# A hybrid decoder layer on one core: the output projection in scaled float16 pairs that are split once, the first operands of the up projection made between its products, the down projection as one sequence of entries

## The chip, the cores and the metric

The kernel runs on one core of one Trainium2 chip, in one launch. The metric is the device time of a launch in microseconds, as the median of several runs. TensorE (PE) multiplies, VectorE (DVE) and ScalarE (ACT) work element by element, GpSimd (POOL) does some elementwise work and issues some transfers, SyncE (SP) issues most DMA transfers. Each engine works through its own list of instructions in order.

## What is computed

One layer on 2048 tokens of width 1024, in float32. The reference, cut to what matters here:

```python
h = rmsnorm(x, norm1_g) * (1 + sc1) + sh1
proj = h @ w_in
q, k, v, fg, xin, bg, cg = jnp.split(proj, IN_SPLITS, axis=-1)
...
attn = forgetting_attention(q, k, v, logf).reshape(b, s, ATTN_WIDTH)
conv = bg * causal_dwconv(cg * xin, conv_mix_w)
mixed = jnp.concatenate([attn, conv], axis=-1)
x = x + g1 * (mixed @ w_out)

h2 = rmsnorm(x, norm2_g) * (1 + sc2) + sh2
u = causal_dwconv(h2 @ w_up, ffn_conv_w)
u_gate, u_val = jnp.split(u, 2, axis=-1)
y = (jax.nn.silu(u_gate) * u_val) @ w_down
return x + g2 * y
```

Attention has 8 heads of 64 over a width of 512, the convolution the other 512 channels; w_out is 1024 x 1024, w_up 1024 x 5632, w_down 2816 x 1024.

## The kernel before, in words

A float32 product is made as three products of halves: each operand is split into a high part (ACT, a copy to the narrower type) and a low part (DVE, the operand less the high part), and `mm3` (L141) issues high x high, high x low and low x high. In the projections and in the output and down projections the halves are of type fp32r, in the up projection float16. A matmul has a stationary tile of 128 x 128 and streams 512 columns.

The program runs through these stages: the norm of x, the input projection (`project`, first K, then Q, then the convolution's channels), attention in 64 steps of two query blocks, the output projection, norm 2, and then twice (hv = 0, 1, half of the rows each) the up projection with the gated convolution, and the down projection.

**The output projection** (`mixed`) has 64 entries: four groups Q of 512 rows, two halves hf of the columns, eight slices k of the depth. For each entry `split` (ACT L720, DVE L721) splits the gated slice of w_out and the slice of the mixed rows anew, 128 splits of 128x512 in all, and four row tiles t take one `mm3` each: 768 matmuls. The first eight entries run under the last steps of attention. At the end of a half the sum is added to x on DVE (L792) and POOL stores the rows (L794, L796) to `x1_sc` in DRAM.

**Norm 2** (`norm2`) makes the up projection's operands. `columns` transposes four 128x128 blocks on PE into PSUM (L1047), ACT applies scale and shift (L1049), `operand` splits into float16 halves (L1037, L1038). Rows of groups 0 and 1 are normalised on POOL (L1075), those of 2 and 3 on DVE (L1077). Its generator is advanced at chosen entries of `mixed`: 18 steps in the output projection. Four more steps, `norm2_rest`, which transposes four column sets a second time, are advanced inside the first iteration of `up(0)`.

**The up projection** (`up`) takes 22 iterations per half, one for each pair of column blocks, and makes the 2048-row product by a scheme with seven products instead of eight: `product` (L1167) issues 12 matmuls each. The weights of iteration i + 1 are loaded (SP, L1126) and made during iteration i: scaled on ACT (L1132), added and subtracted on DVE (L1107, L1108), split by ACT (L1111) and DVE (L1114). Those of iteration 0 are made at the head of `up`. ACT copies the first product's sum (p1, L1216) before the next product goes on accumulating in the same place; DVE adds (L1107); the convolution's taps are on ACT (L1175) and DVE (L1180); `finish` of iteration i runs in iteration i + 1, that of the last one behind the loop.

**The down projection** (`down`) is called four times for each half, 22 entries each; an entry loads a slice of y and of w_down (SP, L1262, L1263), splits both (L720, L721) and feeds four row tiles. At the end each row tile is multiplied by the gate and added to the rows, which are loaded from `x1_sc` at that point (L1026, L1028, L1029). In the first half norm2(2) and norm2(3) follow the first two calls.

**The order of the work.** K(...) pins an instruction: pinned instructions of one engine keep the order of the program text. All others are placed by a scheduler that looks at priorities and at when operands are ready. In `before` the splits of `mixed` and `down`, their additions and most of norm 2 are not pinned. Loads and splits are written right ahead of the products that use them. `magnitudes` loads a tile of w_up and adds up its magnitudes on ACT (L590) for the up projection's scale; 88 of these are spread through the input projection.

## Time and profile before

| | us |
|---|---|
| three runs | 2500.55, 2510.44, 2511.32 |
| their median | 2510.44 |
| the profiled execution, its own time | 2507.0 |
| span of its instructions | 2505.3 |
| PE busy | 2388.9 (95%) |
| DVE busy | 1814.0 (72%) |
| ACT busy | 1292.5 (52%) |
| POOL busy | 375.4 (15%) |

The span runs from the first to the last instruction of the trace; the profiled execution is 1.7 us longer. The median of the runs lies 3.4 us above the profiled execution. Busy shares are means over all stages. The attention steps lie before 962 us, the output projection from there to 1169 us, `up(0)` from 1169 to 1577 us, `down(0)` to 1849 us, `up(1)` to 2241 us, `down(1)` to the end.

### The profile page before, as it was taken

The page shows a single profiled execution, that of the slowest core. Times are in us where ns is not written, and L with a number is a line of the kernel's source. Part 1 is how long each engine was busy: PE and PEld are TensorE (multiplying, and loading weights), DVE is VectorE, ACT ScalarE, POOL GpSimd, SP SyncE. Part 2 cuts the span into 40 slices and gives each one's busy share as a digit, 9 for nine tenths or more (in the row PEclk, how much of TensorE's full clock was granted, in tenths as well). Part 3 has the DMA queues.
Part 4 walks back from the last instruction along what each step waited for, and adds up shares of the span by engine and source line. Part 5 has one row for each costly group of instructions (what it writes and reads, how often), then busy time and mean ns, then how long its engine had stood idle before and what let it go on. Part 6 is the DMA issues. An engine that isn't in the chain of part 4 may idle for free. (4 is left out here: it accounts for less than half of the span.)

```text
span 2505.3 us, 38577 instructions
## 1 busy us (share of the span) xinstructions
PE 2388.9 (95%) x14432; PEld 1655.5 (66%) x14432; DVE 1814.0 (72%) x3377; ACT 1292.5 (52%) x2068; POOL 375.4 (15%) x314
## 2 busy tenths in 40 slices
PE   4999999999899889998999999999999999999999
PEld 4988778888677667776444444678764444447887
DVE  7567784342899887676888988667859888885554
ACT  3533443210788776554656566355545555553333
POOL 4210001011577873110000000000000000000000
PEclk9999999999999999999999999999999999999999
DMA  8444786433789997143222222567742222235775
GB/s 237 148 123 127 196 238 182 147 112 89 149 173 184 189 183 196 72 140 123 67 85 85 92 85 93 191 214 235 219 142 92 84 93 84 85 122 168 230 228 186
DMA packets 429348, 368.71 MB, mean 147 GB/s; under 512 B 184336, under 2 KB 328040, under 8 KB 428136
## 3 DMA queue, kind: packets, MB, share of 16 engines
q1 hardware_dynamic: 421976, 349.40, 50.0%
q10 hardware_dynamic: 4752, 8.46, 0.9%
q0 software_dynamic: 2432, 8.39, 0.9%
q8 instruction: 113, 1.85, 0.3%
q14 instruction: 75, 0.61, 0.1%
HBM read 267.54 MB, written 65.08 MB: 133 GB/s over the span
## 5 line engine op out<-in xcount | busy, mean ns | idle before, releaser
L1167 PEld LDWEIGHTS <-pair 128*128 128x128 f16 x3696 | 364.5, 99 | 470.2 <-issue 36.4
L1167 PE MATMUL acc<-t,pair 128*128 128x512 f16 x2112 | 482.5, 382 | 6.5 <-DVE t L1107 6.5
L1167 PE MATMUL acc<-b,pair 128*128 128x512 f16 x1584 | 372.5, 386 | 17.2 <-DVE pair L1114 6.6
L141 PE MATMUL acc<-hi 128*128 128x512 f32 x960 | 378.5, 395 | 7.9 <-ACT hi L720 5.7
L141 PE MATMUL acc<-hi,lo 128*128 128x512 f32 x960 | 375.8, 391 | 0.2 <-DVE lo L721 0.2
L141 PE MATMUL acc<-lo,hi 128*128 128x512 f32 x960 | 375.1, 391 | 0.0
L721 DVE TENSOR_TENSOR lo<-raw,hi 128x1024 fp32r<-128x1024 f32 (+1 forms) x208 | 236.3, 1142 | 178.8 <-ACT hi L720 178.6
L720 ACT ACTIVATE hi<-raw 128x1024 fp32r<-128x1024 f32 (+1 forms) x208 | 204.9, 991 | 240.4 <-PE acc L141 207.7
L1180 DVE SCALAR_TENSOR_TENSOR w<-w,fcw,w 128x1024 f32<-128x1024 f32 x176 | 226.1, 1285 | 39.9 <-ACT w L1175 30.8
L141 PEld LDWEIGHTS acc<-hi 128*128 128x128 f32 x960 | 180.7, 188 | 48.2 <-ACT hi L720 6.8
L141 PEld LDWEIGHTS acc<-hi,lo 128*128 128x128 f32 x960 | 180.6, 188 | 39.7 <-DVE lo L721 1.5
L141 PEld LDWEIGHTS acc<-lo,hi 128*128 128x128 f32 x960 | 180.6, 188 | 37.0 <-DVE lo L721 0.8
L1111 ACT ACTIVATE pair<-raw 128x1024 f16<-128x1024 f32 x132 | 138.2, 1049 | 70.9 <-DVE raw L1108 70.9
L1175 ACT ACTIVATE w<-w,fcw 128x1024 f32<-128x1024 f32 x88 | 100.7, 1144 | 131.9 <-DVE w L1107 131.9
L879 ACT ACTIVATE s_t<-s_t,nb,cst 128x2048 f32<-128x2048 f32 (+15 forms) x128 | 164.7, 1288 | 5.7
L1114 DVE TENSOR_TENSOR pair<-raw,pair 128x1024 f16<-128x1024 f32 x132 | 160.7, 1219 | 3.9 <-ACT pair L1111 3.9
L590 ACT ACTIVATE wx<-wx 128x512 f32<-128x512 f32 x88 | 55.6, 632 | 202.1 <-DMA wx<-in_w_up_dram 192.5
L141 PE MATMUL pr<-hh,wh 128*128 128x512 f32 x384 | 153.9, 401 | 0.0
L141 PE MATMUL pr<-hh,wl 128*128 128x512 f32 x384 | 151.5, 394 | 2.1 <-DVE wl L178 2.1
L141 PE MATMUL pr<-hl,wh 128*128 128x512 f32 x384 | 151.6, 395 | 0.0
L891 POOL TENSOR_TENSOR wide<-s_t,wide 128x1024 f16<-128x1024 f32 x64 | 136.8, 2138 | 5.3
L862 DVE CUSTOM_DVE_ANT_0 s_t<-ps,nf,mx 128x512 f32<-128x512 f32 (+1 forms) x192 | 119.2, 643 | 16.3 <-PE ps L841 8.0
(278 smaller groups left out, 4568.6 us busy)
## 6 DMA issues: line engine op xcount, KB each, us to landing
raw<-in_w_up_dram SPq DMA_DIRECT2D x88, 512.0 KB, 3.7
raw<-y_sc SPq DMA_DIRECT2D x176, 256.0 KB, 4.3
raw<-in_w_down_dram SPq DMA_DIRECT2D x176, 256.0 KB, 4.3
wx<-in_w_up_dram SPq DMA_DIRECT2D x88, 256.0 KB, 2.8
y_sc<-w SPq DMA_DIRECT2D x44, 512.0 KB, 2.6
wm<-in_w_ada_dram SPq DMA_DIRECT2D x128, 128.0 KB, 2.9
wr<-in_w_in_dram SPq DMA_DIRECT2D x40, 256.0 KB, 4.2
x_t<-in_x_dram SPq DMA_DIRECT2D x16, 512.0 KB, 5.3
```

What stands on the lines that cost most here:

```text
L141: ins = T.matmul(acc, lhsT=a, rhs=b, start=st, stop=sp)
L590: K(A.activation(t, t, AF.Abs, accum_out=l1[:, n : n + 1]))
L720: A.activation(hi, raw, AF.Copy, scale=HS)
L721: V.tensor_tensor(lo, raw, hi.bitcast(F32), op=ALU.subtract)
L862: K(V.tensor_tensor_reduce(out=s_t[:, o0 + c0 : o0 + c0 + cw], in0=ps[:, 0:cw], in1=nf[:, c0 : c0 + cw], scale=1.0, scalar=-3.0e38 if g == ...
L879: K(A.activation(cols, cols, AF.Exp, bias=nb[:, p : p + 1], scale=qk[:, 4:5], accum_out=un["l"][:, p : p + 1]))
L891: K(G.tensor_tensor(wide[:, 1, :], s_t[:, WB * P : WU], wide[:, 0, :], op=ALU.subtract))
L1111: K(A.activation(hi, raw, AF.Copy))
L1114: K(V.tensor_tensor(lo, raw, hi, op=ALU.subtract))
L1167: K(T.matmul(acc, lhsT=a, rhs=b, start=st, stop=sp, skip_group_check=True))
L1175: K(A.activation(y, u[:, 0:1024], AF.Copy, scale=fcw[:, ct : ct + 1]))
L1180: K(V.scalar_tensor_tensor(y, u[:, m : m + 1024], fcw[:, m * 44 + ct : m * 44 + ct + 1], y, op0=ALU.mult, op1=ALU.add))
```

## The change

**Scaled float16 pairs.** `scaled_pair` splits a 128x512 slice into float16 halves after a multiplication by a power of two (ACT L771, DVE L772). The gated w_out is split once (16 slices), the mixed rows once for each group (32 slices): 48 splits instead of 128. `prepare` runs three entries ahead of the products. The addition to x takes the inverse scale in the same DVE instruction (L812); x is loaded for every group as whole rows (L801), and POOL stores 16 whole row tiles of 512 KB (L814).

**The scales.** w_out is loaded and gated four attention steps earlier (steps 28 to 59), and ACT adds up its magnitudes there, one slice in every second step (L736, 16 instructions). DVE takes the largest magnitude of each block of the convolution's result (16 reductions). `out_scales` works out the scales in attention's steps 61 to 63.

**The input projection.** `magnitudes` is left out in three of K's row tiles and three of Q's, and two more are called in the convolution's blocks.

**Norm 2** is pinned throughout, cut into 36 steps, normalises on DVE alone (L1100), and makes `b22` and `t4` with the others; the second transposition goes away. One step is taken per entry of the output projection from entry 17 on; the five steps of the first weights (`first_weights`) follow in the same chain.

**Up and down.** The first weights have a tile of their own; the last iteration of `up` loads and splits the first three pairs of `down`. `down` is one sequence of 88 entries for each half, pinned, with loads six and splits three entries ahead; the rows of the last addition are loaded three entries before the end of a group. The finish of the last `up` iteration, norm2(2), norm2(3) and the next first weights are steps between its entries.

```diff
-                    if k == 3:
+                    if k == 3 and lull[0] <= i < lull[1]:
                         magnitudes()
...
+        last_k = project(AW, gq[:, 1:2], k_hi, k_lo, {0: largest_gains, 1: gain_scales, 3: running_sum, 5: running_offset, 7: largest_value, 9: value_scale}, (0, 13))
+        last_q = project(0, gq[:, 0:1], q_hi, q_lo, {0: last_k, 1: last_k, 3: piece, 6: piece, 9: piece, 12: piece, 15: piece}, (2, 15))
...
+                V.tensor_reduce(vmax[:, 4 * j + ch : 4 * j + ch + 1], y, axis=AX.X, op=ALU.max, apply_absolute_value=True)
...
+        return (
+            lambda: K(G.tensor_tensor(t, t, gates[:, n0 : n0 + 512], op=ALU.mult)),
+            lambda: K(A.activation(wo["junk"][:, 0:512], t, AF.Abs, accum_out=sums[:, n : n + 1])),
...
+    def scaled_pair(tile, raw, scale):
+
+        hi, lo = tile[:, 0:512], tile[:, 512:1024]
+        K(A.activation(hi, raw, AF.Copy, scale=scale))
+        K(V.scalar_tensor_tensor(lo, raw, scale, hi, op0=ALU.mult, op1=ALU.subtract))
+        return hi, lo
+
+    def prepare(Q, hf, i):
+
+        k = order[i]
         if Q == 0:
+            if i % 2 == 0:
+                wp["two"] = fq.tile([P, 2048], F16, tag=("hi", "lo")[hf], name="wp", bufs=4)
+            n0 = i % 2 * 1024
+            wp[k, hf] = scaled_pair(wp["two"][:, n0 : n0 + 1024], wo[k, hf], osc[:, 1:2])
+        if hf == 0:
+            mp[Q, k] = scaled_pair(fb.tile([P, 1024], F16, tag=f"wo{k}{Q % 2}", name="mp"), src[Q, k], osc[:, 0:1])
+            if Q < 3:
+                load_mixed(Q + 1, i)
+
+    def mixed():
+
+        todo = [(Q, hf, i) for Q in range(4) for hf in range(2) for i in range(8)]
+        ready = 0
+        for n, (Q, hf, i) in enumerate(todo):
...
+            while ready < min(n + 3, 64):
+                prepare(*todo[ready])
+                ready += 1
+            if hf == 0 and i == 2:
+                kept[Q] = [wide_temp()[:, 0:D] if Q == 1 else raw_tile() for _ in range(4)]
+                for xp, r in zip(kept[Q], rows):
+                    K(nc.sync.dma_start(xp, x[r, :]))
+            if i == 0:
+                acc = [ps_d.tile([P, 512], F32, tag="d", name="acc") for _ in range(4)]
+            if i != 6:
+                for t in range(4):
+                    for e in (i,) if i < 7 else (6, 7):
+                        a, b = [m[:, t * P : (t + 1) * P] for m in mp[Q, order[e]]]
+                        mm3(acc[t], a, b, *wp[order[e], hf], e == 0, e == 7)
+            if i == 7:
+                for t in range(4):
+                    xp = kept[Q][t][:, n0 : n0 + 512]
+                    K(V.scalar_tensor_tensor(xp, acc[t], oinv, xp, op0=ALU.mult, op1=ALU.add))
+                    if hf:
+                        G.dma_start(x1_sc[Q * 4 + t], kept[Q][t])
+            yield
...
-            if s >= (H - 4) * nu and s % 2 == 0 and s < H * nu:
-                gated = load_out((s - (H - 4) * nu) // 2)
+            if s % 2 == 0 and 28 <= s < 60:
+                gated.append(load_out((s - 28) // 2))
...
+            if s == 61:
+                slow.append(out_scales(ps_x))
...
+            if 28 <= s < 60 and s % 2:
+                gated[-1][0]()
+            if 30 <= s <= 60 and s % 2 == 0:
+                gated[(s - 30) // 2][1]()
...
+            K(A.activation(hi, raw, AF.Copy))
+            K(V.tensor_tensor(lo, raw, hi, op=ALU.subtract))
...
+                for t in range(4):
+                    K(nc.sync.dma_start(xn[Q][t], x1_sc[Q * 4 + t]))
+                yield
...
+                if t % 2:
+                    yield
...
-                    V.tensor_scalar(xn[Q][t], xn[Q][t], ss[:, t : t + 1], None, op0=ALU.mult)
-            yield
+                K(V.tensor_scalar(xn[Q][t], xn[Q][t], ss[:, t : t + 1], None, op0=ALU.mult))
+                if t % 2:
+                    yield
...
+                yield
+                yield
...
-                if Q == 3:
-                    last_operands(Q, k)
-                yield
-
-        def norm2_rest(Q):
-            for k in range(4):
-                operand("b22", k, columns(Q, 4 + k))
+                yield
                 last_operands(Q, k)
...
-            raws = raw_tile(), raw_tile()
+            raws = [raw_tile() if i else fp.tile([P, 1024], F32, tag="first", name="raw", bufs=2) for _ in range(2)]
...
+        def first_weights():
...
+            wts = up_weights(0)
+            ready["ops"] = next(wts)
+            ready["wts"] = wts
+            for _ in range(5):
+                next(wts)
+                yield
...
+        def load_pair(n, i):
...
+        def first_pairs(hv):
+
+            for i in range(3):
+                raws[4 * hv, i] = load_pair(4 * hv, i)
+            yield
+            for i in range(3):
+                pairs[4 * hv, i] = split_pair(raws.pop((4 * hv, i)))
+                yield
+            while True:
+                yield
...
-            wts = up_weights(0)
-            ops = next(wts)
-            for _ in range(5):
-                next(wts)
+            wts, ops = ready.pop("wts"), ready.pop("ops")
...
-                    (ps_d.tile([P, 512], F32, tag="d", name="acc") if i % 2 else ps_u.tile([P, 512], F32, tag="u", name="acc"))
+                    (ps_u.tile([P, 512], F32, tag="u", name="acc") if i % 2 else ps_d.tile([P, 512], F32, tag="d", name="acc"))
...
-                wts = up_weights(i + 1) if i + 1 < NPAIR else iter([None] * 9)
+                wts = up_weights(i + 1) if i + 1 < NPAIR else first_pairs(hv)
...
-            for _ in last:
+            return last
...
+        def down(hv, side):
...
+            todo = [(n, i) for n in range(4 * hv, 4 * hv + 4) for i in range(NPAIR)]
+            loaded = split = 3
+            for e, (n, i) in enumerate(todo):
...
+                while split < min(e + 3, len(todo)):
+                    if loaded == split:
+                        raws[todo[loaded]] = load_pair(*todo[loaded])
+                        loaded += 1
+                    pairs[todo[split]] = split_pair(raws.pop(todo[split]))
+                    split += 1
+                while loaded < min(e + 6, len(todo)):
+                    raws[todo[loaded]] = load_pair(*todo[loaded])
+                    loaded += 1
+                if i == 0:
+                    acc = [ps_d.tile([P, 512], F32, tag="d", name="acc") for _ in range(4)]
+                if i == NPAIR - 3:
+                    xs = [fb.tile([P, 512], F32, tag=f"src{n % 2 * 4 + t}", name="xs") for t in range(4)]
+                    for xp, r in zip(xs, rows):
+                        K(nc.sync.dma_start(xp, x1_sc[r.start // P][:, n0 : n0 + 512]))
...
+                if e < 3 or e % 2 == 0:
+                    next(side, None)
+                if i == NPAIR - 1:
+                    for t in range(4):
+                        add_gated(acc[t], gates[:, D + n0 : D + n0 + 512], xs[t], out[rows[t], n0 : n0 + 512])
+            for _ in side:
                 pass
...
+        steps = {Q: norm2(Q) for Q in range(4)}
+        weights = first_weights()
+        early = chain(steps[0], (None for _ in range(4)), steps[1], weights)
+        for n, _ in enumerate(mix, 8):
+            if n >= 17:
+                next(early, None)
+        for _ in early:
-            up(hv, iter(()) if hv else norm2_rest(1))
+            last = up(hv)
+            down(hv, last if hv else chain(last, steps[2], steps[3], first_weights()))
```

The order of instructions, at three places. ACT at the start of `up(0)`, before (L1132 scales a weight tile of iteration 1, L1216 copies p1, L1049 and L1037 make operands of `norm2_rest`, L1111 splits weights):

```order
L1111 ACTIVATE pair<-raw 128x1024 x2
L1049 ACTIVATE t_15027<-pt,sh_137,a_136 128x512
L1037 ACTIVATE b_15029<-t_15027 128x512
L1037 ACTIVATE t_15036<-t_15032 128x512
L1132 ACTIVATE raw<-raw,cst 128x1024 x2
L1216 ACTIVATE t_15054<-acc 128x512
L1221 ACTIVATE w_15056<-halo 128x2
L1049 ACTIVATE t_15077<-pt,sh_137,a_136 128x512
L1037 ACTIVATE b_15079<-t_15077 128x512
```

and in the change (L1152 scales, L1271 is p1, L1130 splits weights):

```order
L1058 ACTIVATE t_14710<-t_14706 128x512
L1152 ACTIVATE raw<-raw,cst 128x1024 x2
L1130 ACTIVATE pair<-raw 128x1024
L1130 ACTIVATE pair<-t_14739 128x512
L1130 ACTIVATE pair<-raw 128x1024 x2
L1152 ACTIVATE raw<-raw,cst 128x1024 x2
L1271 ACTIVATE t_14862<-acc 128x512
L1276 ACTIVATE w_14864<-halo 128x2
L1276 ACTIVATE w_14865<-halo 128x2
L1284 ACTIVATE w_14864<-acc 128x512
```

The operands of norm 2 are gone from between the copies; the two scale operations of iteration 1 still stand ahead of p1.

SP at the same place, in the change, with what each row waits for (DMASW are transfers that POOL issued, here the stores of `x1_sc`; L801 loads x of group 3, L1146 loads w_up, the third and fourth L1146 row those of iteration 1):

```order
L801 DMA raw<-in_x_dram 128x1024 [waits DMAHW5_49,DMASW3_49,DVE_49]
L1146 DMA raw<-in_w_up_dram 128x8x128 [waits DVE_49]
L1146 DMA raw<-in_w_up_dram 128x8x128 [waits DMAHW1_49,DMAHW6_49,DMASW4_49,DVE_49]
L1146 DMA raw<-in_w_up_dram 128x8x128 [waits DMAHW2_49,DMAHW7_49,DMASW5_49,DVE_49]
L1146 DMA raw<-in_w_up_dram 128x8x128 [waits DMAHW0_49,DVE_49]
```

and before:

```order
L1126 DMA raw<-in_w_up_dram 128x8x128 [waits DMAHW2_49,DVE_49]
L1126 DMA raw<-in_w_up_dram 128x8x128 [waits DMAHW4_49,DVE_49]
L1126 DMA raw<-in_w_up_dram 128x8x128 [waits DMAHW5_49,DVE_49]
```

The loads of iteration 1 now go to tiles that hold rows of group 3, so they wait for the stores of its first two row tiles.

DVE in the last iteration of `up(0)`, before (L721 splits pairs of `down`, L1107 and L1108 are additions and subtractions of `up`):

```order
L721 TENSOR_TENSOR lo<-raw,hi 128x1024
L1108 TENSOR_TENSOR raw<-t_17956,raw 128x512
L721 TENSOR_TENSOR lo<-raw,hi 128x1024
L1108 TENSOR_TENSOR raw<-raw 128x512
L1114 TENSOR_TENSOR pair<-t_17956,pair 128x512
L1107 TENSOR_TENSOR t_18032<-t_17957,acc 128x512
L1107 TENSOR_TENSOR w_17966<-t_18032,t_18018 128x512
```

and in the change (L1198 splits, L1126 adds, L1239 taps, L1251 the product of the two halves of u):

```order
L1126 TENSOR_TENSOR t_17875<-t_17851,acc 128x512
L1198 TENSOR_TENSOR lo<-raw,hi 128x1024
L1251 TENSOR_TENSOR w_17853<-w_17806,w_17853 128x1024
L1198 TENSOR_TENSOR lo<-raw,hi 128x1024 x2
L1126 TENSOR_TENSOR t_17930<-t_17851,acc 128x512
L1126 TENSOR_TENSOR w_17860<-t_17930,t_17916 128x512
```

Three splits remain ahead of the additions, at written places; the weights of the next `up` no longer stand among them.

## Rows read from the trace of the kernel before

**Rows 1.** The page, busy time of the engines over the span.

```profile
PE 2388.9 (95%) x14432; PEld 1655.5 (66%) x14432; DVE 1814.0 (72%) x3377; ACT 1292.5 (52%) x2068; POOL 375.4 (15%) x314
```

**Rows 2.** Chain of waits, a piece of down(1): start us, us, what.

```profile
2382.65 114.09 PE acc L141 x501
```

**Rows 3.** Timeline of PE, mid up(0): start us, us, operation, [idle before <-releaser].

```profile
1385.55 2.75 PE L1167 MATMUL acc<-b,pair 128*128 128x512 f16 x12
1388.14 2.75 PE L1167 MATMUL acc<-t,pair 128*128 128x512 f16 x12
```

**Rows 4.** Windows, output projection: stretch, us, PE PEld DVE ACT POOL, PEclk, DMA, GB/s.

```profile
991.00:1169.27 178.27, 169.41 (x759) 136.99 (x757) 119.16 (x204) 96.73 (x166) 23.50 (x31) 0.99 0.37 128
```

**Rows 5.** Timeline of PE, an idle stretch of the output projection.

```profile
1085.75 0.50 PE L141 MATMUL acc<-hi 128*128 128x512 f32 x1 [1.99 <-ACT hi L720]
```

**Rows 6.** Windows: the first 60 us of up(0), and 60 us in its middle.

```profile
1169.27:1229.27 60.00, 46.41 (x193) 20.50 (x193) 46.59 (x60) 32.16 (x47) 0.91 (x2) 0.86 0.18 58
1380.00:1440.00 60.00, 60.00 (x280) 27.20 (x279) 53.91 (x62) 35.45 (x53) 0.00 (x0) 1.00 0.27 88
```

**Rows 7.** Timeline of PE: end of up(0), start and end of up(1).

```profile
1572.79 4.42 PE L1167 MATMUL acc<-t,pair 128*128 128x512 f16 x10 [3.18 <-DVE t L1107]
...
1852.74 4.45 PE L1167 MATMUL acc<-b,pair 128*128 128x512 f16 x10 [3.58 <-DVE pair L1114]
...
2236.83 4.44 PE L1167 MATMUL acc<-t,pair 128*128 128x512 f16 x12 [3.35 <-DVE t L1107]
```

**Rows 8.** Windows around these three places.

```profile
1560.00:1580.00 20.00, 16.82 (x66) 6.86 (x65) 19.21 (x21) 9.79 (x14) 0.00 (x0) 0.83 0.56 177
1849.16:1889.16 40.00, 36.42 (x156) 15.99 (x157) 30.56 (x38) 19.75 (x27) 0.00 (x0) 0.91 0.26 81
2200.00:2240.00 40.00, 36.65 (x165) 16.25 (x163) 36.48 (x41) 24.94 (x33) 0.00 (x0) 0.97 0.42 132
```

**Rows 9.** Windows: K to Q projection, the convolution's blocks, attention.

```profile
240.00:260.00 20.00, 15.98 (x72) 11.97 (x70) 14.74 (x56) 10.50 (x24) 1.88 (x3) 1.00 0.58 157
260.00:280.00 20.00, 19.87 (x84) 15.82 (x85) 13.27 (x46) 8.90 (x19) 1.85 (x3) 0.91 0.71 191
...
380.00:420.00 40.00, 40.00 (x179) 32.70 (x178) 15.73 (x32) 10.48 (x28) 3.63 (x5) 1.00 0.54 163
...
680.00:700.00 20.00, 18.71 (x291) 14.43 (x289) 18.99 (x62) 17.10 (x34) 12.92 (x8) 1.00 0.94 154
```

**Rows 10.** Timeline of PE, idle stretches at the start of up(0).

```profile
1172.85 3.82 PE L1167 MATMUL acc<-b,pair 128*128 128x512 f16 x10 [2.97 <-DVE pair L1114]
1184.63 5.17 PE L1167 MATMUL acc<-b,pair 128*128 128x512 f16 x12 [4.50 <-ACT t L1216]
1201.97 5.03 PE L1167 MATMUL acc<-b,pair 128*128 128x512 f16 x12 [6.12 <-ACT t L1237]
```

**Rows 11.** Timeline of ACT at the start of up(0), scale operations and p1.

```profile
1181.93 2.17 ACT L1132 ACTIVATE raw<-raw,cst 128x1024 f32<-128x1024 f32 x2
1184.01 0.57 ACT L1216 ACTIVATE t<-acc 128x512 f32<-128x512 f32 x1
```

**Rows 12.** DMA issues: out<-in, engine, count, KB each, median us to landing.

```profile
raw<-in_w_up_dram SPq DMA_DIRECT2D x88, 512.0 KB, 3.7
...
x_sc<-raw POOLq DMA_DIRECT2D x4, 512.0 KB, 3.4
...
x_sc<-w POOLq DMA_DIRECT2D x4, 512.0 KB, 5.9
```

**Rows 13.** Timeline of PE, idle stretches in down, first and last of five.

```profile
1669.34 0.30 PE L1047 MATMUL pt<-ident,w 128*128 128x128 f32 x1 [1.13 <-DVE w L1077]
...
2382.65 0.50 PE L141 MATMUL acc<-hi 128*128 128x512 f32 x1 [0.50 <-DVE t L1028]
```

**Rows 14.** Lines by shape, L590 on ACT: count, ns min/median/max, first and last start.

```profile
L590 ACT ACTIVATE wx<-wx x88: 627/632/636, 162.6 to 506.6; 128x512 f32<-128x512 f32 x88
L590 ACT ACTIVATION_READ_ACCUMULATOR wx<-wx x88: 183/187/195, 163.2 to 507.2; 128x1 f32 x88
```

213 lines of the change are left out of this document (78 added, 135 removed).

## The prediction

> **What bounds the kernel now.** The page's busy times come first: PE is busy 95% of the span, DVE 72%, ACT 52% [rows 1]. So time can only be won in two ways: the matmuls themselves get faster, or PE's gaps close. The chain of waits and the timeline give the pace of an undisturbed stream. For fp32r halves it is 114.09 us for 501 matmuls, 227.7 ns each [rows 2]; for float16 halves twelve matmuls start 2.59 us after the twelve before, 215.8 ns each [rows 3]. The gaps are read from the timeline, each with the instruction that ended it, and from windows, where the number of matmuls against an undisturbed stretch also shows what a lowered clock cost. A single number for idle time would miss that: after a long gap the granted clock stands below 1 for a while.
>
> The places with gaps are the output projection (8.9 us of 178.3 without PE, granted clock 0.99 [rows 4]), where PE waits for ACT's splits [rows 5]; the first 60 us of up(0), clock 0.86 [rows 6]; the ends of both ups and the start of up(1) [rows 7, 8]; and the passage from K's projection to Q's [rows 9]. In mid up PE never stops: 280 matmuls in 60 us [rows 6].
>
> **The change part by part.**
>
> *Float16 in the output projection.* 768 matmuls go from 227.7 to 215.8 ns [rows 2, 3]: 768 x 11.9 ns = **9.1 us** won. This is on the path, as PE is the bound there. The stream of [rows 3] alternates weight loads and matmuls of 512 columns, as the new output projection will. The Trainium skill, "TensorE: Matmul & The Clock Gate", section "Back-to-back issue gap", gives about 131 ns for each matmul of just such a sustained stream, by which this term would be 768 x (227.7 - 131) = 74 us, 65 more. The trace does not agree with it, so the measured pace stays in the sum.
>
> *Splits once and three entries ahead.* The gaps and the clock of this stage cost 8.86 us idle and (1 - 0.99) x 178 = 1.8 us, some 10.6 [rows 4]. 48 splits take the place of 128, and an entry's operands are asked for about 3 x 2.6 us before its products. I take **10 us** won. The stage may keep half of it, if the pinned steps of norm 2 hold up a split: the bounds are 5 and 10.6. The first entries carry extra: three pairs must be made, and the scales known, before the first product. This is work of a few hundred ns each beside attention's last steps; I charge 1 us, between 0 and 4.
>
> *Start of up(0).* 193 matmuls run in its first 60 us, of which 16 are the transpositions of four column sets; 177 products against 280 [rows 6] are 103 x 214 ns = 22.1 us lost. Three gaps account for 2.97 + 4.50 + 6.12 = 13.6 of that [rows 10], the rest is the lower clock and the transpositions. The first gap ends on the first weights, the others on ACT copies that stand in ACT's order behind operands of norm 2. With the operands and first weights made earlier, these three causes go. A new one comes: the two scale operations of iteration 1 still stand ahead of p1 (2.17 and 0.57 us [rows 11]), and their loads now wait for stores of x1. The chain behind the second row tile's addition is a store of 3.4 to 5.9 us, a load of 3.7 us [rows 12], the two scale operations and p1: 9.8 to 12.3 us. It begins some 2 us before the projection's last product, since the last twelve products (2.6 us) belong to the tiles behind it. PE has two products of 12, 5.2 us, until it needs p1's copy. So p1 is 2.7 to 5.2 us late; I take the middle, 4.0, and a third of the clock's loss that came with three gaps, (22.1 - 13.6 - 1.7) / 3 = 2.3, where 1.7 is 16 transpositions at about half a matmul. That leaves 6.3, and **15.8 us** won. Bounds: no gap (22.1 won), and a second gap like the third of [rows 10] with its clock loss on top (6.1 + 2.3 = 8.4 less).
>
> *Ends of up and start of up(1).* At the end of up(0) PE idles 3.18 us [rows 7], and 66 matmuls in 20 us against 93.3 [rows 6, 8] are 5.9 us. At up(1)'s start 156 against 186.7 in 40 us are 6.6; at its end 165 against 186.7 are 4.6 [rows 8]. All three end on DVE operations [rows 7], and DVE's order there has splits of the down projection, or weights, ahead of the additions that PE waits for. The new order makes the first weights during down(0), and the first pairs at written places. I take **6 + 6 + 4.6 = 16.6 us**; what could stay is half of the two ends, 5.
>
> *Down.* Five gaps of PE at the passages between its calls are 1.13 + 0.40 + 1.02 + 0.41 + 0.50 ([rows 13], the first and the last of the five), 3.5 us in all. **3.5 us** are won. They end on DVE: the normalised rows, and the gating at the end of a group, which waits for rows loaded only then. Both are asked for earlier now. What was unpinned is pinned, so side steps can delay a split, but splits run three entries, 8 us, ahead.
>
> *Input projection.* Between K and Q PE idles 4.0 of 20 us and the clock stands at 0.91 in the next 20 [rows 9]: 4.0 + 1.8 = 5.8. The change takes `magnitudes` out of this passage; I take **5 us**, between 0 and 5.8. The two put in their place lie in the convolution's blocks, where PE has no gap (40.00 of 40) and ACT is busy 10.5 of 40 us [rows 9]. The same row hides the 16 new reductions on DVE, 15.7 of 40 busy there.
>
> *Sums of w_out's magnitudes.* 16 operations on ACT in attention, 632 + 187 ns by the nearest row [rows 14], 13.1 us in all. Attention has DVE busy 19.0, PE 18.7 and ACT 17.1 of 20 us [rows 9]: ACT has slack but not at every moment. A fifth to a quarter shows: 3 us lost, between 0 and 13.1. The loads and gating of w_out only move four steps, on SP and POOL.
>
> **The sum**: 9.1 + 10 - 1 + 15.8 + 16.6 + 3.5 + 5 - 3 = 56.0. The profiled execution took 2507.0, so it becomes 2451.0; that execution lies 3.4 below the median of the runs.
>
> **The rivals.**
>
> 1. *Up(0) starts as late as before*: the three gaps come back with other names (scale operations behind x1's stores, p1 behind them). For it: the waits in SP's order. Against it: two of the three gaps had norm 2's operands for cause, and these are gone. Then only the transpositions' 1.7 us are won there: 2451 + 14.1 = 2465.
>
> 2. *ACT becomes the bound in attention*: all 16 sums show, 10.1 more: 2461. For it: 17.1 of 20 us. Against it: DVE is fuller.
>
> 3. *The change does not do what it says*: float16 streams no faster in this stage than fp32r, since its tiles and places in memory differ from those of up. 2451 + 9.1 = 2460. Against it: the stream of [rows 3] has the same shape.
>
> 4. *Slower.* The pinned steps of norm 2 stall PE, as the four in up(0) did. There they came with 22.1 - 1.7 = 20.4 us, 5.1 each [rows 6]. Now 36 stand pinned between the entries of the output projection, and every one puts several DVE and ACT operations ahead of the splits. At that price the gain of 56 is gone from the 11th stalled step on; all 36 would give 2451 + 184 = 2635. Against it: 18 such steps in the same stage before came with no more than the 10.6 us of that whole stage [rows 4], 0.6 each, and DVE is busy 119 of 178 there, ACT 97.
>
> 5. *The stream is paced by its weight loads alone*: they take 27.20 us for 279, 97.5 ns each [rows 6]. If the matmuls of the output projection overlapped so far, 768 x (215.8 - 97.5) = 91 us more would be won: 2360. Against it: PE has nothing else to wait for in [rows 3] and keeps 215.8. The page named above points this way, with 131 ns and so 2386.
>
> **How the numbers follow.** The forecast of 2451 has 0.69, rival 1 0.13, rival 2 0.08, rival 3 0.04, rival 4 0.05, rival 5 0.01. A measurement of this kernel tells about 0.5%, 12.6 us, from no change, so faster means below 2498. All cases but rival 4 lie there: faster 0.95. Rival 4 with 9 to 13 stalled steps is no change, 0.02, with more slower, 0.03.
>
> The range's lower end takes the forecast with no gap at up(0) (-6.3), free sums (-3) and start (-1), the last of the output projection's and the K to Q passage's gaps (-0.6 and -0.8) and the spread of the runs below the profiled execution (2507.0 - 2500.6 = 6.4): 2507.0 less 56.0, 6.3, 3, 1, 1.4 and 6.4 is 2433, and 2430 with a little for idle time in other stages. The upper end takes rival 1 (+14.1), half of the output projection's gaps (+5), half of the ups' ends (+5) and the spread above (2511.3 - 2507.0 = 4.3), or rival 2 with two of these: 2478. Outside lie rivals 4 and 5, 0.06, and about 0.1 of the tails.
>
> **What would show it.** Right: the output projection with some 216 ns per matmul and hardly a gap; up(0) beginning with one gap before the second product with b21, ended by ACT's p1, of 3 to 5 us; no gap of over 1 us at the ends of up; some 25 matmuls more than the 72 + 84 of the 40 us between K and Q; attention longer by 0 to 5 us. Wrong: gaps in the output projection that end on a split with norm 2's operations ahead of it on the same engine; two or more gaps at up(0); attention's steps longer wherever a sum of magnitudes stands; gaps in down ended by a split.

## The result and the profile after

The changed kernel takes 2469.53 us (median of 4 runs, 2467.69 to 2473.61) against 2508.31 (4 runs, 2500.55 to 2511.32): ratio 0.9852, 95% interval 0.9826 to 0.9879, some 39 us or 1.5% less. The forecast of 2451 had 56 us. The time lies in the range, the way is right, and a third of the expected gain did not come.

The profiled execution of the change has a span of 2467.1 us against 2505.3. The place of each stage's first matmul in the timelines says where the 38.2 us lie. (The stage boundaries named ahead of the prediction, 1577 and 2241 us, are the last gaps inside up; by the timeline up(0) ends at 1596.2 and up(1) at 2259.1, and that is used here.)

| stage | before | after | won | forecast |
|---|---|---|---|---|
| up to the first score of attention | 634.4 | 633.2 | 1.2 | 5 |
| attention and output projection | 534.9 | 531.0 | 3.9 | 15.1 |
| up(0) | 426.9 | 406.2 | 20.7 | 21.8 |
| down(0) | 252.3 | 253.9 | -1.6 | 3.5 with down(1) |
| up(1) | 410.5 | 398.7 | 11.8 | 10.6 |
| down(1) | 246.2 | 244.2 | 2.0 | see down(0) |

Both ups came as forecast. Of the missing part 15 us lie ahead of them and 3.1 in the two downs. The page's busy times, which answer to [rows 1]:

```profile
PE 2364.3 (96%) x14419; PEld 1585.8 (64%) x14419; DVE 1790.0 (73%) x3333; ACT 1256.6 (51%) x2016; POOL 358.6 (15%) x298
```

PE's timeline, the pace of the output projection and all its gaps of over 1 us from the end of attention to up(0) (start us, us, operation, idle before and what ended it):

```profile
966.11 0.21 PE L954 MATMUL po<-v,near 128*128 128x64 f16 x1 [4.37 <-DVE at L962]
973.88 2.74 PE L142 MATMUL acc<-wp,mp 128*128 128x512 f16 x6 [2.69 <-ACT mp L771]
...
1103.88 10.52 PE L142 MATMUL acc<-wp,mp 128*128 128x512 f16 x48
1114.24 0.60 PE L1068 MATMUL pt<-ident,w 128*128 128x128 f32 x4
1117.78 4.03 PE L142 MATMUL acc<-wp,mp 128*128 128x512 f16 x12 [2.94 <-DVE raw L812]
...
1143.43 16.81 PE L142 MATMUL acc<-wp,mp 128*128 128x512 f16 x77 [1.18 <-DVE raw L812]
...
1175.41 4.22 PE L1226 MATMUL acc<-b,pair 128*128 128x512 f16 x12 [5.89 <-ACT t L1271]
```

Forty-eight matmuls take 1114.24 - 1103.88 = 10.36 us, 215.8 ns each: the pace of [rows 3] to the digit. So the float16 term is there, and the loss stands in the brackets. None of these five waits ends on a split of a pair that was asked for too late, except the second, at the very start. Windows of the same places as [rows 6, 8, 9] (stretch, us, PE, PEld, DVE, ACT, POOL, clock, DMA share, GB/s):

```profile
240.00:260.00 20.00, 17.26 (x75) 13.63 (x74) 14.70 (x53) 9.02 (x20) 2.60 (x4) 0.92 0.52 132
260.00:280.00 20.00, 18.98 (x87) 14.97 (x86) 16.84 (x60) 8.31 (x15) 1.85 (x3) 0.99 0.62 171
...
1164.90:1224.90 60.00, 54.11 (x245) 24.17 (x244) 41.40 (x49) 30.05 (x44) 0.53 (x1) 0.94 0.38 117
1560.00:1580.00 20.00, 20.00 (x92) 12.67 (x91) 16.40 (x17) 10.35 (x13) 0.00 (x0) 1.00 0.50 158
1824.40:1864.40 40.00, 40.00 (x187) 18.13 (x185) 32.49 (x38) 20.37 (x28) 0.00 (x0) 1.00 0.21 70
2200.00:2240.00 40.00, 40.00 (x184) 24.47 (x182) 30.05 (x30) 18.11 (x22) 0.00 (x0) 1.00 0.53 164
```

The last three are gapless, at full clock. Up(0)'s first 60 us have 245 matmuls against 280: 35 x 214 ns = 7.5 us lost, where 22.1 were. Between K and Q 75 + 87 = 162 matmuls run against 72 + 84 = 156 [rows 9]: hardly any of the 5 us came.

### The profile page after: what moved, and what is told of

Read it like the earlier page. It is cut to its first block, busy times and chain, and to the rows that moved or that the text cites. A ratio compares the mean times of both kernels' runs of the same rounds, so it can differ in the third digit from the quotient of the medians.

```text
span 2467.1 us, 38327 instructions
## 1 busy us (share of the span) xinstructions
PE 2364.3 (96%) x14419; PEld 1585.8 (64%) x14419; DVE 1790.0 (73%) x3333; ACT 1256.6 (51%) x2016; POOL 358.6 (15%) x298
## 4 chain that ended last, share of the span: by engine, by line
PE 77%; DVE 7%; DMA 6%; issue 5%; ACT 3%; POOL 1%; SPq 1%; ACTq 0%; DVEq 0%; POOLq 0%
PE acc L1226 32%; PE acc L142 24%; PE pr L142 10%; PE pv L142 3%; DMA far<-wide 3%; PE pt L918 1%; PE ps L857 1%; PE ps L858 1%; DVE near L925 1%; PE po L954 1%; DVE s_t L881 1%; DMA wx<-in_w_up_dram 1%; PE po L956 1%; PE po L955 1%; ACT s_t L898 1%
## 5 line engine op out<-in xcount | busy, mean ns | idle before, releaser
L1226 PE MATMUL acc<-b,pair 128*128 128x512 f16 x1584 | 364.9, 380 | 5.9 <-ACT t L1271 5.9
L1198 DVE TENSOR_TENSOR lo<-raw,hi 128x1024 fp32r<-128x1024 f32 x176 | 211.7, 1223 | 141.9 <-ACT hi L1197 141.1
L142 PE MATMUL acc<-hi 128*128 128x512 f32 x704 | 276.9, 393 | 3.4 <-DVE t L1049 3.4
L142 PE MATMUL acc<-lo,hi 128*128 128x512 f32 x704 | 274.3, 390 | 0.3 <-DVE lo L1198 0.3
L142 PE MATMUL acc<-hi,lo 128*128 128x512 f32 x704 | 274.2, 389 | 0.0
L1197 ACT ACTIVATE hi<-raw 128x1024 fp32r<-128x1024 f32 x176 | 181.8, 1054 | 163.8 <-PE acc L142 131.1
L1239 DVE SCALAR_TENSOR_TENSOR w<-w,fcw,w 128x1024 f32<-128x1024 f32 x176 | 226.1, 1285 | 34.6 <-ACT w L1234 25.3
L142 PE MATMUL acc<-wp,mp 128*128 128x512 f16 x768 | 172.2, 383 | 6.9 <-DVE raw L812 4.1
L1130 ACT ACTIVATE pair<-raw 128x1024 f16<-128x1024 f32 x132 | 138.2, 1049 | 69.1 <-DVE raw L1127 69.1
L1133 DVE TENSOR_TENSOR pair<-raw,pair 128x1024 f16<-128x1024 f32 x132 | 160.8, 1219 | 6.8 <-ACT pair L1130 6.8
L142 PEld LDWEIGHTS acc<-hi 128*128 128x128 f32 x704 | 132.1, 188 | 34.1 <-DVE t L1049 5.5
L142 PEld LDWEIGHTS acc<-hi,lo 128*128 128x128 f32 x704 | 132.2, 188 | 27.7
L142 PEld LDWEIGHTS acc<-lo,hi 128*128 128x128 f32 x704 | 132.2, 188 | 27.4 <-DVE lo L1198 0.7
```

What stands on the lines that cost most here:

```text
L142: ins = T.matmul(acc, lhsT=a, rhs=b, start=st, stop=sp)
L1130: K(A.activation(hi, raw, AF.Copy))
L1133: K(V.tensor_tensor(lo, raw, hi, op=ALU.subtract))
L1197: K(A.activation(hi, raw, AF.Copy))
L1198: K(V.tensor_tensor(lo, raw, hi.bitcast(F32), op=ALU.subtract))
L1226: K(T.matmul(acc, lhsT=a, rhs=b, start=st, stop=sp, skip_group_check=True))
```

## The experiments

Stage lengths below are from the first matmul of a stage to that of the next, in each kernel's own timeline. One caution holds for all: stages ahead of the output projection vary between executions with the same code. Attention's 64 normalisations (the DVE line that writes `at`, one for each step) run from 656.1 to 981.7 us in the trace of before and from 654.5 to 985.1 in that of the first experiment below, which has the same attention: 325.6 against 330.6. In the traces that have the change's attention they take 333.8 (the change itself) to 342.8 us, and the first score comes at 628.4 to 637.1 us where the code up to it is the change's. So a verdict on a part rests on its own stage, not on the total alone.

Where attention varies can be read from the same line, and its end does not:

| from normalisation to normalisation, us | before | float16 alone | change | no scales | two orders | four orders |
|---|---|---|---|---|---|---|
| 1st to 49th | 251.4 | 257.1 | 250.8 | 255.5 | 255.8 | 252.9 |
| 49th to 57th | 39.8 | 39.8 | 40.4 | 40.4 | 40.4 | 46.0 |
| 57th to 64th | 34.4 | 33.7 | 42.6 | 37.7 | 42.7 | 37.8 |

The 57th and the 64th, in the kernel before and in the change:

```profile
947.29 0.29 DVE L943 TENSOR_TENSOR at<-po,l 128x128 f32<-128x128 f32 x1
981.68 0.28 DVE L943 TENSOR_TENSOR at<-po,l 128x128 f32<-128x128 f32 x1
```

```profile
946.80 0.29 DVE L962 TENSOR_TENSOR at<-po,l 128x128 f32<-128x128 f32 x1
989.38 0.29 DVE L962 TENSOR_TENSOR at<-po,l 128x128 f32<-128x128 f32 x1 [1.58 <-PE po L956]
```

In the eight traces with the scales at steps 61 to 63 the last row is 42.4 to 43.6. So the end of attention became some 8 us longer by the change, and of these the scales make up some 5: without them it takes 37.7. The other 3 were not tried apart; the first pairs are made there.

**Float16 alone, in the kernel before.**

```diff
-                (mh, ml), (wh, wl) = halves(pair_tiles())
-                split(wo[k, hf], wh, wl)
-                split(src[Q, k], mh, ml)
+                (mh, ml), (wh, wl) = halves([fq.tile([P, 2048], F16, tag=n, name=n, bufs=4) for n in ("hi", "lo")])
+                for raw, hi, lo in ((wo[k, hf], wh, wl), (src[Q, k], mh, ml)):
+                    A.activation(hi, raw, AF.Copy)
+                    V.tensor_tensor(lo, raw, hi, op=ALU.subtract)
```

> The kernel before with one part of the change alone: the pairs of the output projection are float16 (unscaled), still split 128 times at the old places. Theory 'the pace is the float16 gain': 768 matmuls at 216 instead of 227 ns, 8 to 9 us less than before (2508.3 to about 2500), and the stalls of the output projection that end on splits stay (8 to 10 us). Rival 'the splits bound this stage': PE waits longer for the same splits, and less than 3 us is won.

Measured: 2499.96 against 2510.64 in the same session, ratio 0.9963 (0.9948 to 0.9978), 5.5 to 13 us. The largest wait on a split is still there, as in [rows 5]:

```profile
996.15 0.39 PE L141 MATMUL acc<-hi 128*128 128x512 f16 x1 [2.13 <-ACT hi L769]
```

The ratio comes to 9.3 us, so the float16 term of 9.1 us is confirmed apart from all else in the change. In its own stage, from the first product to up(0), it is 196.4 us instead of 203.0, 6.6 less, since PE's waits there grew from 9.0 to 10.8 us.

**No scales to work out.** The constant 1 takes the place of `out_scales`.

```diff
-            if s == 61:
-                slow.append(out_scales(ps_x))
+            if s == 30:
+                G.memset(osc, 1.0)
+                G.memset(oinv, 1.0)
```

> The changed kernel without working out the scales of the output projection: they are the constant 1, and the twelve DVE and two PE operations of attention's last steps are left out; the sums of w_out's magnitudes on ACT and the reductions of the convolution's blocks stay. Theory 'the scales stand in DVE's order ahead of the last scores': PE's idle 4.4 us at the end of attention shrinks to below 2, the wait of 2.7 us for the first pairs stays, and the time falls by 3 to 4 us from the 2469.5 of the change. Rival 'the first pairs are late whatever the scales': the idle time moves to the first product, which then waits 5 us or more, and the time stays within 1 us.

Measured: 2467.27 (2465.68 to 2469.27), ratio to before 0.9833 (0.9813 to 0.9853); span 2463.9, 3.2 less. PE's timeline at the end of attention:

```profile
962.65 0.19 PE L954 MATMUL po<-v,near 128*128 128x64 f16 x1 [1.54 <-DVE at L962]
...
969.39 0.61 PE L142 MATMUL acc<-wp,mp 128*128 128x512 f16 x2 [3.20 <-ACT mp L771]
```

In the kernel before, the first of these waits was

```profile
962.06 0.19 PE L935 MATMUL po<-v,near 128*128 128x64 f16 x1 [1.68 <-DVE at L943]
```

The first wait falls from 4.37 to 1.54, what before had there; the second stays, a little longer. The first theory holds for both waits; the median is 2.3 us lower where it had 3 to 4. What it leaves is a start that waits 3.2 us for pairs in any case. Where the 4.9 us at the end of attention (42.6 to 37.7) come from is in the trace of the change: the twelve small DVE operations take 4.6 us in all, 1.97 of them in one. DVE and POOL at that place:

```profile
960.68 0.26 DVE L755 TENSOR_SCALAR rim<-rim 128x2 int32<-128x2 int32 x1
960.97 0.17 DVE L756 RECIPROCAL rim<-rim 128x2 f32<-128x2 f32 x1
961.17 1.97 DVE L757 TENSOR_SCALAR rim<-rim 128x2 int32<-128x2 int32 x1
...
963.65 0.73 DVE L881 CUSTOM_DVE_ANT_0 s_t<-ps,nf,mx 128x512 f32<-128x512 f32 x1
```

```profile
960.99 2.12 POOL L910 TENSOR_TENSOR wide<-s_t,wide 128x1024 f16<-128x1024 f32 x1
```

The same masking of 256 numbers takes 0.26 us at 960.68 and 1.97 at 961.17, and the second ends at 963.14, with POOL's operation (963.11). The scores (L881) stand behind it. This is taken up again in the last experiment.

**p1 ahead of the weights' scale operations.**

```diff
-                wts = up_weights(i + 1) if i + 1 < NPAIR else first_pairs(hv)
-                ops = next(wts)
                 p1 = temp()
                 K(A.activation(p1, X, AF.Copy))
+                wts = up_weights(i + 1) if i + 1 < NPAIR else first_pairs(hv)
+                ops = next(wts)
```

> The changed kernel with two statements of the up projection in the other order: the copy p1 is issued before the next iteration's weights are begun, so that it stands ahead of their two scale operations on ACT. Theory 'p1 is late because it stands behind the scale operations, which wait for w_up, which waits for stores of x1': the 5.9 us of idle and the slow clock behind it at the start of up(0) go, 7 us less (2469.5 to about 2462.5). Rival 'the weights of iteration 1 are late anyway': PE waits at a later product of iteration 0 or 1 for a weight pair or an addition, 4 to 6 us, and no more than 3 us are won.

Measured: 2484.30 (2482.68 to 2486.70), 15 us slower than the change. The gap at up(0)'s start is gone as expected, but neither theory had what came instead. PE waits in 41 of the 44 iterations, on the addition of p1 and Y:

```profile
1258.33 2.75 PE L1226 MATMUL acc<-t,pair 128*128 128x512 f16 x12 [0.33 <-DVE t L1126]
1276.95 2.75 PE L1226 MATMUL acc<-t,pair 128*128 128x512 f16 x12 [0.33 <-DVE t L1126]
```

An iteration takes 1276.95 - 1258.33 = 18.62 us. In the change p1 comes every 18.13 us, by ACT's timeline:

```profile
1265.14 0.60 ACT L1271 ACTIVATE t<-acc 128x512 f32<-128x512 f32 x1
1283.27 0.60 ACT L1271 ACTIVATE t<-acc 128x512 f32<-128x512 f32 x1
```

44 x 0.49 = 21.6 us lost, 7 won: 14.6. By the stages up(0) takes 3.1 and up(1) 9.8 us longer, 12.9; the rest of the 15 lies ahead of the ups, in what varies between executions. The scale operations head the weights' chain (ACT scales, DVE adds and subtracts, ACT and DVE split), and DVE's later additions for PE stand behind that chain in its order. An order that costs once at the start pays 44 times in the loop.

**Additions freed from norm 2's steps.**

```diff
-        early = chain(steps[0], (None for _ in range(4)), steps[1], weights)
+        early = chain(steps[0], steps[1], weights)
         for n, _ in enumerate(mix, 8):
-            if n >= 17:
+            if n >= 17 and n % 8 != 6 and not 30 <= n < 31:
```

> The changed kernel with norm 2's steps kept away from the last entry of each half in the output projection (no step after the seventh of eight entries; the four empty steps between the two groups are used up instead). Theory 'the additions at the end of a half stand behind norm 2's pinned operands on DVE, whose ACT halves come late': the waits of 2.9 and 1.2 us that end on these additions go, with the slow clock behind them 4 to 6 us less than 2469.5. Rival 'the additions wait for the accumulators themselves, since only four exist': the waits stay, within 1 us.

Measured: 2461.84 (2457.23 to 2465.61), ratio to before 0.9805 (0.9778 to 0.9833), 7.7 less than the change. Windows, the change first, then this kernel:

```profile
1080.00:1160.00 80.00, 74.23 (x352) 35.02 (x350) 50.84 (x75) 28.60 (x42) 2.12 (x4) 0.98 0.21 79
```

```profile
1080.00:1160.00 80.00, 78.56 (x378) 37.22 (x377) 56.78 (x86) 29.93 (x44) 3.11 (x6) 1.00 0.27 100
```

PE's idle time in these 80 us falls from 5.8 to 1.4 us. From the output projection's first product to up(0) it is 183.6 us instead of 190.3. The first theory holds. In the change DVE's timeline shows the place: the pinned split of a norm 2 operand waits for its ACT half, and the four additions that free the accumulators follow it all at once.

```profile
1115.70 0.69 DVE L1059 TENSOR_TENSOR t<-t,t 128x512 f16<-128x512 f32 x1 [0.69 <-ACT t L1058]
1116.31 0.75 DVE L772 SCALAR_TENSOR_TENSOR mp<-src,rim,mp 128x512 f16<-128x512 f32 x1
1116.98 2.72 DVE L812 SCALAR_TENSOR_TENSOR raw<-acc,rim,raw 128x512 f32<-128x512 f32 x4
```

**No sums of w_out's magnitudes.**

```diff
-            if 30 <= s <= 60 and s % 2 == 0:
-                gated[(s - 30) // 2][1]()
+            if s == 30:
+                G.memset(sums, 16.0)
```

> The changed kernel without the sixteen sums of w_out's magnitudes on ACT during attention; in their place the constant 16 is written once, and the scales are still worked out from it at the same place. Theory 'the sums hardly show, DVE sets attention's pace': attention's steps keep their length, and the time falls by 0 to 3 us from 2469.5. Rival 'ACT is the bound there': up to 13 us less.

Measured: 2470.08 (2468.65 to 2472.05), ratio to before 0.9852 (0.9827 to 0.9877), that of the change. The rival's 13 us are excluded: ACT's slack [rows 9] takes the sums, or nearly so. A cost of up to some 3 us could hide in the spread of these runs.

**Fewer of w_up's magnitudes in K's projection.**

```diff
-... 9: value_scale}, (0, 13))
+... 9: value_scale}, (0, 6))
...
         l1 = bp.tile([P, 88], F32, name="l1", bufs=1)
+        V.memset(l1, 0.0)
```

> The changed kernel with w_up's magnitudes summed in six of K's row tiles instead of thirteen; the fourteen tiles of w_up that drop out are left out of the sum, which is cleared first. Theory 'ACT falls behind in K's projection because each sum waits some 3.5 us for its load, two per row tile of 5.6 us, and Q's first weights stand behind the last of them': the passage from K to Q loses 2 us or less instead of 6.9, and the time falls by 4 to 5 us. Rival 'Q's weights are late for their own loads': the idle time there stays at 4 us or more and ends on weights whose load came late.

Measured: 2471.02 (2467.20 to 2473.28): in the total nothing. In its own stage, windows as above:

```profile
240.00:260.00 20.00, 18.73 (x89) 14.92 (x87) 16.54 (x56) 8.56 (x16) 1.86 (x3) 1.00 0.49 126
260.00:280.00 20.00, 20.00 (x95) 16.33 (x94) 16.21 (x57) 7.60 (x15) 2.48 (x4) 1.00 0.56 152
```

184 matmuls in these 40 us against 162 in the change: 22 x 20 / 95 = 4.6 us; K and Q take 195.8 us instead of 200.6. So the first theory holds for the place. That the total did not follow is within attention's own spread: attention and output projection took 540.2 us in this trace, 531.0 in that of the change, and 8 of these 9 us lie between the first and the 49th normalisation (258.8 against 250.8). The cut of three row tiles that the change made was too short, since ACT is still behind when K ends.

**Side steps away from the ends of down's groups.**

```diff
-                if e < 3 or e % 2 == 0:
+                if (e < 3 or e % 2 == 0 or i == 3) and i < NPAIR - 2:
                     next(side, None)
```

> The changed kernel with the side steps of down kept away from the last two entries of each group (they are taken after the fourth entry instead). Theory 'norm 2's pinned steps hold up the additions at the end of a group in down(0)': of the 7 us that PE loses in down(0) at least 3 go, 2469.5 to about 2466. Rival 'the accumulators of the next group are the limit, whatever the steps': the waits on the gating operation stay, within 1 us.

Measured: 2476.16 (2472.28 to 2482.38). Down(0) itself takes 254.1 us, in the change 253.9; attention is the longer part here too. In the change PE waits on the additions, for example

```profile
1761.49 0.47 PE L142 MATMUL acc<-hi 128*128 128x512 f32 x1 [1.16 <-DVE t L1049]
```

and here on splits in their place:

```profile
1597.86 0.49 PE L142 MATMUL acc<-hi 128*128 128x512 f32 x1 [1.75 <-ACT hi L1197]
1599.12 0.50 PE L142 MATMUL acc<-lo,hi 128*128 128x512 f32 x1 [0.77 <-DVE lo L1198]
```

Neither theory holds: the waits leave the additions, so the accumulators are not the limit, but they come back elsewhere. Where 2 to 3 us of down(0) could be had stays open.

**Without the two prefetches.**

```diff
-            down(hv, last if hv else chain(last, steps[2], steps[3], first_weights()))
+            down(hv, last if hv else chain(last, steps[2], steps[3]))
...
+            if hv:
+                for _ in first_weights():
+                    pass
             wts, ops = ready.pop("wts"), ready.pop("ops")
...
-                wts = up_weights(i + 1) if i + 1 < NPAIR else first_pairs(hv)
+                wts = up_weights(i + 1) if i + 1 < NPAIR else iter([None] * 9)
...
-            loaded = split = 3
+            loaded = split = 0
```

> The changed kernel with two pieces of the change undone: the first weights of up(1) are made at the head of up(1), not during down(0), and the first three pairs of down are loaded and split in down, not in up's last iteration. Theory 'these two prefetches are what closed the gaps at the ends of up and at the start of up(1)': up(1)'s start loses 8 to 12 us (load 3.7, two scale operations 2.2, an addition, two splits), each down's start 6 to 9 us, 22 to 30 us in all, 2469.5 to 2492 to 2500. Rival 'the pinned order alone closed them, the prefetches are for the rest': less than 8 us in all.

Measured: 2482.44 (2479.05 to 2484.21), 13 us more than the change; up(1) takes 6.2 us longer, down(0) 3.1, up(0) 0.9 and down(1) 1.0: 11.2. PE at the start of up(1) and of down(0):

```profile
1831.54 3.23 PE L1226 MATMUL acc<-b,pair 128*128 128x512 f16 x10 [3.60 <-DVE pair L1133]
...
1571.56 0.50 PE L142 MATMUL acc<-lo,hi 128*128 128x512 f32 x1 [0.76 <-DVE lo L1198]
```

The first row is the wait of before [rows 7] back, 3.60 against 3.58. The waits on DVE's additions in up's last iterations do not come back. So between the theories: the prefetch of weights is worth what up(1)'s start lost, and the gaps near the ends of up were not closed by the prefetch of pairs. That leaves the pinned order, which was not tried by itself.

**Two orders together.** The freed additions, and p1 first in iteration 0 alone.

```diff
                 p1 = temp()
+                if i == 0:
+                    K(A.activation(p1, X, AF.Copy))
...
                 ops = next(wts)
+                if i:
+                    K(A.activation(p1, X, AF.Copy))
```

> The changed kernel with norm 2's steps kept away from the last entries of each half, as in the run that freed these additions, and p1 ahead of the scale operations in iteration 0 of each up alone. The run with p1 first everywhere lost about 0.5 us in each of 44 iterations and lost no time at the start of up(0). Theory 'only the first iteration has anything to win, the others want the weights first': up(0) takes 7 us less than its 406.2 and up(1) stays at 398.7, so with the freed additions 13 to 14 us less than 2469.5, about 2456. Rival 'iteration 1 pays for it': up(0) falls by less than 4 us.

Measured: 2459.84 (2456.05 to 2464.56), ratio to before 0.9809 (0.9793 to 0.9825). Up(0) 399.5 instead of 406.2, up(1) 398.7, the output projection 183.6: each stage as the first theory has it, 13.4 us together. ACT at the start of up(0):

```profile
1169.33 0.60 ACT L1270 ACTIVATE t<-acc 128x512 f32<-128x512 f32 x1 [6.62 <-PE acc L1226]
1175.14 2.19 ACT L1152 ACTIVATE raw<-raw,cst 128x1024 f32<-128x1024 f32 x2 [5.21 <-DMA raw<-in_w_up_dram]
```

The weights come no sooner; ACT now waits for them alone. The median is 9.7 us below that of the change. The profiled execution, the slowest of the five, has K, Q and attention 8 us longer than that of the change.

**Four orders together.** In addition the scales four steps earlier (steps 24 to 57 for 28 to 61), and eight of w_up's sums moved from K to the convolution.

```diff
-... 9: value_scale}, (0, 13))
+... 9: value_scale}, (0, 8))
...
-                    if j < 3 or (ch, name) == (0, "x"):
+                    if j < 3 or ch == 0:
                         magnitudes()
+                    if j < 2 and name == "b":
+                        magnitudes()
```

> The same kernel with two more moves: w_out's loads, gating and sums four attention steps earlier still, so that the scales are worked out from step 57 on, and eight of the sums of w_up's magnitudes moved from K's last row tiles into the convolution's blocks (none left out). Theory 'the scales cost time only in the last steps, where they hold up the last scores': from the first attention product to the start of up(0) it takes 3 us less than in the kernel with two orders; K's stage takes 4 us less than 200.6; in all 6 to 8 us less, about 2449. Rival 'DVE sets the pace of every attention step, so the scales cost the same wherever they stand': no gain from the first move; and for the second, that ACT's backlog is only moved: K's stage shorter, the convolution's longer by as much.

Measured: 2453.36 (2452.74 to 2454.68), ratio to before 0.9785 (0.9772 to 0.9799): the fastest here, 16 us below the change. K and Q take 195.6 us, 5 less than in the change, the convolution 277.2 against 275.9: the first theory for that move. For the scales the rival holds. From attention's first score to up(0) it is 527.4 us against 529.4 with two orders, a difference below attention's own spread, so this sum alone would not decide. The table of normalisations does: the last seven steps take 4.9 us less (37.8 for 42.7) and the eight before them, where the scales now stand, 5.6 more (46.0 for 40.4). The cost has moved with them, and so has PE's wait; its timeline there:

```profile
941.46 0.38 PE L859 MATMUL ps<-kh,qs 128*128 128x512 f16 x1 [2.04 <-DVE mx L883]
```

**One masking less.** On top of the last kernel:

```diff
         K(V.reciprocal(osc, osc))
-        K(V.tensor_scalar(bits, bits, 0x7F800000, None, op0=ALU.bitwise_and))
-        K(V.tensor_scalar(osc, osc, 16384.0, None, op0=ALU.mult))
+        K(A.activation(osc, osc, AF.Copy, scale=16384.0))
```

> The kernel with four orders and one change to how the scales are worked out: the second masking of the reciprocal on DVE is left out (the reciprocal of a power of two has no mantissa to mask) and the multiplication by 16384 is done on ACT. In the four runs looked at, that masking of 128x2 numbers took 1.97 us on DVE and ended with POOL's 2.1 us operation beside it, while the same form took 0.25 us a moment earlier. Theory 'DVE waits for POOL there, and what stands behind it, the last scores, is late': the scales take DVE 2 us less, PE's wait at that attention step falls by 1.5 to 2 us, 2453.4 to about 2451.5. Rival 'something else on DVE is hit by the same POOL operation instead': another DVE instruction there takes 1.5 us more, and the time stays within 1 us.

Measured: 2454.43 (2450.39 to 2457.74), no gain. PE's wait at that step is 1.50 us instead of 2.04. The rival's mechanism is there; DVE, then POOL:

```profile
938.58 1.74 DVE L760 TENSOR_TENSOR rim<-rim 128x1 f32<-128x1 f32 x1 [0.27 <-ACT rim L759]
```

```profile
938.16 2.13 POOL L911 TENSOR_TENSOR wide<-s_t,wide 128x1024 f16<-128x1024 f32 x1
```

A product of two columns, 0.16 us in the change's trace, now takes 1.74 and ends (940.32) with POOL's operation (940.29).

## Why the prediction was right, and where it was off

*Float16, 9.1 us.* Right: 215.8 ns in the changed kernel, and 5.5 to 13 us in the run with nothing else, 6.6 in its own stage. The rule of the Trainium skill ("TensorE: Matmul & The Clock Gate", "Back-to-back issue gap"), about 131 ns, is not borne out by this stream either.

*"Splits once and three entries ahead", 10 won, "between 0 and 4" charged for the start, of which 1.* This is the step that failed. The cause that the prediction priced, late splits, went. Two others came. The pinned steps of norm 2 delay the additions that free the accumulators: 6.7 us, won back by moving the steps. That is rival 4's mechanism, at the ends of a half only, not at 11 steps. And the start was mis-sized: with the 3 us set for the sums the prediction had attention 4 us longer, and its last seven steps alone became 8.2 us longer (34.4 to 42.6). 4.9 of these are the scales, which hold up the last scores (PE waits 4.37 us where it waited 1.68 before); 3.3 are the rest of the start, where the first product waits 2.69 us for its pair. The prediction took the scales for work of a few hundred ns beside attention's last steps. But DVE is the fullest engine there [rows 9], and the twelve operations took 4.6 us of it.

*Start of up(0), 15.8 won.* Right in kind: one gap, ended by p1 behind the scale operations. It was 5.89 us, not 4.0, and with the clock 7.5 us were lost, not 6.3. The chain of waits names the sum's wrong term, a load of 6.64 us where 3.7 were set [rows 12]:

```profile
1165.95 6.64 DMA raw<-in_w_up_dram
```

The store ahead of it is as the prediction had it, 3.0 us to landing where 3.4 to 5.9 were set. The chain puts the load's release down to a DVE split (L1133), but that split ends after the load was issued. What released it was the store of x1's second row tile, which landed 0.06 us before the issue, at 1165.89. DVE's split, POOL's store, and the store's time to landing:

```profile
1165.05 1.22 DVE L1133 TENSOR_TENSOR pair<-raw,pair 128x1024 f16<-128x1024 f32 x1
```

```profile
1162.84 0.53 POOL L814 DMA_DIRECT2D x_sc<-raw  x1 [0.77 <-DVE raw L812]
```

```profile
DMA to landing us min/median/max: 3.0/3.0/3.0
```

SP's wait for this store ended at 1165.91. In SP's order shown ahead of the prediction, the two loads of iteration 1 are therefore the second and third L1146 row, those that wait for the first two stores. How much of the 6.64 us is due to the other stores and loads under way beside it was not tried.

*Ends of up and start of up(1), 16.6 won.* Right: no gap is left in any of the three windows. The run without prefetches shows that the prefetch of weights closed the gap at up(1)'s start, and that the prefetch of pairs was not needed at the ends.

*Down, 3.5 won.* Off in down(0): the three of the five gaps that lie there went, 2.5 us, and others of 0.3 to 1.2 us came with the pinned side steps, 3.7 us; the stage takes 1.6 us more. In down(1), without norm 2's steps, 2.0 were won.

*Input projection, 5 won.* Off by almost all of it. The step that failed is "the change takes `magnitudes` out of this passage": it took out three row tiles, and ACT's backlog outlasts them: K and Q went from 201.3 to 200.6 us. Six tiles with sums instead of thirteen won 4.6 us at the place.

*Sums of w_out's magnitudes, 3 lost.* Inside its bounds of 0 and 13.1: nothing shows, and 3 us is about the most that the runs could hide.

Together: 11.2 us missed in attention and the output projection, 3.8 ahead of it, 3.1 in down. The 11.2 are not attention's spread: up to the 57th normalisation both traces took 291.2 us from the first. They are the 6.7 us of the additions and the 8.2 us of attention's end, less the 4 us that the forecast had charged, 10.9. The bounds had a held-up split in the output projection and up to 4 us for the start; neither is what came, so that the time lies in the range is in part luck. (The upper end by its own terms is 2479.4, not 2478; nothing hangs on it.)

## What to carry to other kernels

A pinned order stalled PE here where an operation that frees an accumulator stood behind side work with a round trip to another engine. Keeping side steps out of the entries that end an accumulation won 6.7 us in the output projection; in down(0) it won nothing, as the waits moved to splits. Where a stage starts slowly because of an order that serves its loop, change the order in the first iteration alone. Small operations on the engine that sets a stage's pace cost their full time, with what a neighbour adds to it, and moving them within the stage moves the cost: 4.2 to 4.6 us of operations made attention's steps 4.9 to 5.6 us longer at either place.

## What had not been expected of the hardware

Some DVE instructions on 128x1 or 128x2 numbers, all in SBUF, lasted until a POOL operation ended that was running when they began. In the nine traces that have it, the second masking took 1.97 or 1.98 us and ended within 0.04 us of POOL's product; when it was taken out, the two-operand product in its place took 1.74 us instead of 0.16. Not every DVE instruction is held: in the trace of the change the reciprocal of 128x2 (L928) took 0.16 us in the 44 cases that began during a POOL operation as in the 20 others, and the scores (L881), which read PSUM, took as long beside POOL as without it. The Trainium skill ("SBUF — State Buffer", "SBUF: two separate sides") has a port pair that DVE and POOL share, locked for a whole instruction, for DVE's two-port modes or two operands in SBUF; the masking and the product agree with it. The profile names no releaser for these waits, so the ports as their cause are not shown by the rows, only the common end.
